# Weight buffers in the feed-forward: four raw and three split, in place of two and four, and pure blocks first in a seven-product piece

## The chip, the cores and the metric

One core of one Trainium2 chip runs the whole program. The metric is device time in microseconds (us) of one execution; lower is better. Engines are named as the profile names them: PE (TensorE, matmuls), PEld (its weight loads), DVE (VectorE), ACT (ScalarE), POOL (GpSimd) and SP (SyncE, which issues most transfers, its queue being written SPq). Every engine takes its instructions in a fixed order, laid down when the program is built.

## The reference

A decoder trunk of two layers on 256 tokens of width 2048, all in float32. Layer 0 mixes tokens with a diagonal state-space model and a gated linear unit, layer 1 with sliding-window attention; each is followed by a SwiGLU feed-forward of inner width 5632:

```python
def swiglu(x, w_gate, w_up, w_down):
    return (jax.nn.silu(x @ w_gate) * (x @ w_up)) @ w_down

for i in range(DEPTH):                       # DEPTH = 2
    hn = rmsnorm(h, norm_mix[i])
    mix = s5_mixer(hn, ...) if i == 0 else sliding_window_attention(hn, ...)
    h = h + mix
    hn = rmsnorm(h, norm_ffn[i])
    h = h + swiglu(hn, ffn_w_gate[i], ffn_w_up[i], ffn_w_down[i])
return rmsnorm(h, norm_final)
```

## The kernel before

**Pieces.** All large weights are read once, in pieces of 1 MB: four blocks of 128 x 512 float32. `W.src` lists the pieces in the order in which PE uses them (32 of the gated unit, 132 of the first feed-forward, 20 and 16 of the attention, 132 of the second feed-forward). A piece goes through two kinds of buffers. SP loads it into a *raw* buffer (`load`). ACT and DVE then split it into a high part rounded to fp32r and a low part, the rest (`split`), which lie in a *place*, a tile `w` of twice the size. A float32 product is three fp32r matmuls: x high with w high, x high with w low, x low with w high (`three`, `products`).

**Plain pieces.** `high` and `low` split a plain piece with one ACT instruction (L130) and one DVE instruction (L135). It feeds 24 matmuls.

**Seven-product pieces.** In gate and up a piece holds 2 x 2 blocks (two blocks of rows; up and gate). In about half of them the 2 x 2 block product is formed from seven block products instead of eight. `sevenths` makes four sums of blocks on DVE (`sf`, L144 to L146), splits these into the place `w` (L148 on ACT, L149 on DVE, in two halves), and splits three of the blocks themselves, the pure blocks, into a tile `sd` (L148, L149). There is one buffer `sd` and one buffer `sf`. Such a piece feeds 21 matmuls. `ORDER` sets the order of the seven products; m1, c11 and c12 read `sd`, the other four read `w`.

**Chunks.** A feed-forward is worked in 11 chunks of 512 inner columns. `gu(c)` does gate and up of a chunk in 8 pieces, numbered p0 to p7 here; from chunk 2 on p0, p2, p4 and p6 are seven-product pieces. `sums` and the lines after the loop then put the products together on DVE (L1213 to L1216, L1240, L1243, L1244), and the result `act` is transposed on DVE into `bt` (L1042), sent through DRAM by POOL, and split as `hT` (L1256 on ACT, L1257 on DVE). The down products of the group of chunks before lie between the chunks: 4 plain pieces after a chunk, d0 to d3 here, whose sums go into `h` (L1266). After chunks 0 and 1 there are none, and 12 stand at the end. One chunk with its downs is 12 pieces.

**Lookahead.** When PE's part of piece i is written, `next` has the splits written up to piece i + 3 in the feed-forward (i + 2 elsewhere) and the loads two pieces beyond. There are two raw buffers, and four places in the feed-forward (three elsewhere). The fourth place lies in the feed-forward's own pool `W.pool`. A build-time scheduler sorts what is ready into the fixed order of each engine, so that order is not quite that of the code.

Of the kernel before, what the change touches and what calls it, by code (L numbers as in the profile page):

```python
# [9 lines left out]
F32 = mybir.dt.float32  # L10
# [7 lines left out]
P = 128  # L18
# [40 lines left out]
def kernel(  # L59
# [9 lines left out]
    def nm(s):  # L69
        uid[0] += 1  # L70
        return f"{s}_{uid[0]}"
# [5 lines left out]
    pp = ctx.enter_context(tc.tile_pool(name="pp", bufs=4))  # L77
    wq = ctx.enter_context(tc.tile_pool(name="wq", bufs=2))
# [14 lines left out]
    class Weights:  # L93
# [11 lines left out]
        def load(self, upto):  # L105
            while len(self.raw) < min(upto, len(self.src)):
                i = len(self.raw)
                aps = self.src[i][0]
                t = pp.tile([P, 4, 512], F32, tag="raw", name=nm("raw"), bufs=2)
                v = t.rearrange("p (k s) n -> p s k n", s=len(aps))  # L110
                for s, ap in enumerate(aps):
                    nc.sync.dma_start(v[:, s], ap.rearrange("(a p) n -> p a n", p=P))  # L112
                self.raw.append(t)

        def place(self, i):

            if i in (1, 4):
                return self.third()
            if not self.src[i][2]:
                self.wide = None  # L120
                pool, n = (wp, 1) if i % 3 == 1 else (wq, 2)
            else:
                self.wide = i % 3 if self.wide is None else self.wide + 1
                pool, n = {1: (wp, 1), 3: (self.pool, 1)}.get(self.wide % 4, (wq, 2))
            return pool.tile([P, 2, 4, 512], F32R, tag="w", name=nm("w"), bufs=n)

        def high(self, i, keep=lambda ins: ins):
# [34 lines left out]
        def next(self):  # L162
            i = self.used
            self.used += 1
            n = 4 if self.src[min(i + 3, len(self.src) - 1)][2] and i + 3 < self.limit else 3
            self.split(min(i + n, self.limit))
            self.load(i + n + 2)
            return self.hl[i]

    W = Weights()  # L170
# [65 lines left out]
    def s5(early_piece):  # L236
# [3 lines left out]
        with st:  # L240
# [591 lines left out]
            def outputs(q, mms=(0, 1), keep=lambda ins: ins):  # L832
                for mm in mms:
                    for i in range(4):
                        for ri in range(2):
                            for h in range(2):
                                place = 8 * mm + 4 * h + i
                                for g2 in range(2):
                                    r = rows(g2)
                                    keep(PE.matmul(py[q][g2][h * NK : (h + 1) * NK, mm, i], St[q][r, ri, place],  # L840
                                                   Tt[q][r, place, ri].rearrange("p j c -> p (j c)"),
                                                   start=False, stop=mm == 1 and i == 3 and ri == 1))
                                    keep = lambda ins: ins
# [341 lines left out]
    def swiglu(norm, out_norm):  # L1185
# [3 lines left out]
        def three(acc, x_, w, first, last):  # L1189
# [3 lines left out]

        M = {"m1": ("a11", "b11"), "c11": ("a12", "b21"), "c12": ("s4", "b22"), "c21": ("a22", "t4"),
             "m5": ("s1", "t1"), "m6": ("s2", "t2"), "m7": ("s3", "t3")}
        ORDER = ("m1", "m6", "m7", "m5", "c11", "c21", "c12")

        def gu(c):
            acc = {}
# [3 lines left out]
            def to(m):  # L1203
                first = m not in acc
                if first:
                    acc[m] = bank([P, 512], "acc")
                return acc[m], first
# [10 lines left out]
            for p in range(8):  # L1218
                w = W.next()
                xt = norm.xt[p // 2]  # L1220
                if p in sv:
                    for m in ORDER:
                        a, first = to(m)
# [245 lines left out]
    wp = ctx.enter_context(tc.tile_pool(name="wp", bufs=1))  # L1469
# [11 lines left out]
    glu(n0)  # L1481
    n1 = Norm(1, (), (0, 1, 2, 3))
    swiglu(n0, n1)
    ffn.close()
    n2 = Norm(2, (0, 1, 2, 3))
    attention(n1, n2, ffn_pool)
    swiglu(n2, Last(None))
    ffn.close()

# [27 lines left out]
```

## Time and profile before

| | us |
|---|---|
| median of 3 runs | 2003.87 (2003.23 to 2007.51) |
| profiled execution, its own time | 2004.44 |
| its span in the trace | 2002.3 |
| PE, DVE, ACT busy | 1909.4, 1594.4, 1001.8 |
| first feed-forward, first to last matmul | 295.45 to 1024.25 |
| second feed-forward, first to last matmul | 1259.85 to 1993.35 |

The span begins with the state-space part and the gated unit (to 295 us); the attention lies between the two feed-forwards. A row of the trace begins with the start in us and the duration; "idle before" is how long the engine stood still, with the instruction that released it. Matmuls overlap in the pipeline, so the time of one (389 ns) is longer than the step from one start to the next.

### The profile page before, as it was taken

The page shows a single profiled execution, that of the slowest core. Times are in us where ns is not written, and L with a number is a line of the kernel's source. Part 1 is how long each engine was busy: PE and PEld are TensorE (multiplying, and loading weights), DVE is VectorE, ACT ScalarE, POOL GpSimd, SP SyncE. Part 2 cuts the span into 40 slices and gives each one's busy share as a digit, 9 for nine tenths or more (in the row PEclk, how much of TensorE's full clock was granted, in tenths as well). Part 3 has the DMA queues.
Part 4 walks back from the last instruction along what each step waited for, and adds up shares of the span by engine and source line. Part 5 has one row for each costly group of instructions (what it writes and reads, how often), then busy time and mean ns, then how long its engine had stood idle before and what let it go on. Part 6 is the DMA issues. An engine that isn't in the chain of part 4 may idle for free.

```text
span 2002.3 us, 25614 instructions
## 1 busy us (share of the span) xinstructions
PE 1909.4 (95%) x10050; PEld 1556.1 (78%) x10050; DVE 1594.4 (80%) x1933; ACT 1001.8 (50%) x1061; POOL 217.6 (11%) x272
## 2 busy tenths in 40 slices
PE   7789999999999999999999999999999999999998
PEld 6678887877777777777888778877777877787786
DVE  8965568888888888888687887888888888888875
ACT  6554455454444544444465555645444444454443
POOL 6840000100000000000020111001000000000000
PEclk9799999999999999999999999999999999999999
DMA  4037775665566566655785866656666566755664
GB/s 129 24 103 235 241 225 190 228 229 190 192 229 214 186 199 221 214 185 196 242 277 185 265 207 230 213 203 222 206 209 227 173 210 210 225 177 202 215 227 151
DMA packets 201084, 405.76 MB, mean 203 GB/s; under 512 B 16418, under 2 KB 16482, under 8 KB 200836
## 3 DMA queue, kind: packets, MB, share of 16 engines
q1 hardware_dynamic: 185984, 356.88, 53.8%
q0 software_dynamic: 14144, 45.12, 7.0%
q10 hardware_dynamic: 836, 2.14, 0.3%
q8 instruction: 78, 1.28, 0.3%
q14 instruction: 42, 0.34, 0.1%
HBM read 379.45 MB, written 24.64 MB: 202 GB/s over the span
## 4 chain that ended last, share of the span: by engine, by line
DVE 32%; DMA 32%; PE 20%; ACT 10%; issue 5%; SPq 1%; POOL 0%; ACTq 0%; DVEq 0%; POOLq 0%
DMA raw<-in_ffn_w_gate_dram 19%; DVE w L135 13%; DMA raw<-in_ffn_w_down_dram 11%; ACT w L130 8%; PE acc L964 5%; PE acc L966 5%; PE acc L965 5%; DVE sd L149 4%; DVE w L149 3%; DVE sf L144 2%; SPq L112 1%; DVE scan L615 1%; ACT sd L148 1%; DVE sf L146 1%; DVE sf L145 1%
## 5 line engine op out<-in xcount | busy, mean ns | idle before, releaser
L135 DVE TENSOR_TENSOR w<-raw,w 128x2048 fp32r<-128x2048 f32 x248 | 570.1, 2299 | 222.3 <-ACT w L130 220.1
L130 ACT ACTIVATE w<-raw 128x2048 fp32r<-128x2048 f32 x250 | 478.7, 1915 | 406.9 <-DMA raw<-in_ffn_w_down_dram 174.7
L1191 PE MATMUL acc<-w,xT 128*128 128x512 f32 x1080 | 426.6, 395 | 27.7 <-DVE w L149 27.4
L1190 PE MATMUL acc<-w,xT 128*128 128x512 f32 x1080 | 424.0, 393 | 4.5 <-DVE u L1240 2.0
L148 ACT ACTIVATE w<-sf 128x1024 fp32r<-128x1024 f32 x164 | 172.3, 1052 | 301.7 <-DVE sf L144 288.1
L965 PE MATMUL acc<-w,hT 128*128 128x512 f32 x704 | 274.1, 389 | 1.1 <-DVE w L135 1.1
L1192 PE MATMUL acc<-w,xT 128*128 128x512 f32 x704 | 274.1, 390 | 0.0
L966 PE MATMUL acc<-w,hT 128*128 128x512 f32 x704 | 273.9, 389 | 0.0
L964 PE MATMUL acc<-w,hT 128*128 128x512 f32 x704 | 273.9, 389 | 0.0
L1191 PEld LDWEIGHTS acc<-w,xT 128*128 128x128 f32 x1080 | 204.3, 189 | 81.5 <-DVE w L149 39.5
L1036 POOL DMA_DIRECT2D pd<-bt x160 | 88.1, 554 | 1521.6 <-DVE bt L1042 1431.6
L1190 PEld LDWEIGHTS acc<-w,xT 128*128 128x128 f32 x1080 | 204.0, 189 | 53.0 <-ACT w L148 4.9
L149 DVE TENSOR_TENSOR w<-sf,w 128x1024 fp32r<-128x1024 f32 x164 | 199.6, 1219 | 1.8 <-ACT w L148 1.6
L144 DVE TENSOR_TENSOR sf<-raw 128x1024 f32<-128x1024 f32 x82 | 100.3, 1223 | 112.9 <-DMA raw<-in_ffn_w_gate_dram 112.9
L148 ACT ACTIVATE sd<-raw 128x1536 fp32r<-128x1536 f32 x82 | 121.3, 1480 | 113.8 <-DMA raw<-in_ffn_w_gate_dram 91.2
L965 PEld LDWEIGHTS acc<-w,hT 128*128 128x128 f32 x704 | 132.2, 188 | 29.3 <-DVE w L135 1.9
L1192 PEld LDWEIGHTS acc<-w,xT 128*128 128x128 f32 x704 | 132.4, 188 | 27.8
L964 PEld LDWEIGHTS acc<-w,hT 128*128 128x128 f32 x704 | 132.2, 188 | 27.4
L966 PEld LDWEIGHTS acc<-w,hT 128*128 128x128 f32 x704 | 132.2, 188 | 27.4
L1192 PE MATMUL acc<-w,xs 128*128 128x512 f32 x376 | 149.0, 397 | 0.0
L149 DVE TENSOR_TENSOR sd<-raw,sd 128x1536 fp32r<-128x1536 f32 x82 | 143.8, 1754 | 2.1 <-ACT sd L148 0.9
L1191 PE MATMUL acc<-sd,xT 128*128 128x512 f32 x246 | 99.0, 402 | 18.9 <-DVE sd L149 18.9
(281 smaller groups left out, 2676.2 us busy)
## 6 DMA issues: line engine op xcount, KB each, us to landing
raw<-in_ffn_w_up_dram SPq DMA_DIRECT2D x176, 512.0 KB, 3.9
raw<-in_ffn_w_gate_dram SPq DMA_DIRECT2D x176, 512.0 KB, 5.0
raw<-in_ffn_w_down_dram SPq DMA_DIRECT2D x88, 1024.0 KB, 5.1
raw<-in_s_w_glu_dram SPq DMA_DIRECT2D x32, 1024.0 KB, 5.3
raw<-in_attn_w_qkv_dram SPq DMA_DIRECT2D x20, 1024.0 KB, 5.4
pd<-bt POOLq DMA_DIRECT2D x136, 128.0 KB, 4.0
act<-pd POOLq DMA_DIRECT2D x34, 512.0 KB, 4.8
raw<-in_attn_w_o_dram SPq DMA_DIRECT2D x16, 1024.0 KB, 5.1
```

What stands on the lines that cost most here:

```text
L130: keep(S.activation(w[:, 0], self.raw[i], AF.Copy))
L135: keep(e.tensor_tensor(lo, self.raw[i], hi.bitcast(F32), op=ALU.subtract))
L144: V.tensor_tensor(f[:, 0:2], bc(r[:, 0], 1, 2), r[:, 1:3], op=ALU.subtract)
L148: S.activation(v[1], v[0], AF.Copy)
L149: V.tensor_tensor(v[2], v[0], v[1].bitcast(F32), op=ALU.subtract)
L964: keep(PE.matmul(acc, x_[:, 0], w[0][:, a], start=first, stop=False))
L965: PE.matmul(acc, x_[:, 0], w[1][:, a], start=False, stop=False)
L966: PE.matmul(acc, x_[:, 1], w[0][:, a], start=False, stop=last)
L1036: nc.gpsimd.dma_start(d[t].rearrange("(q k) e -> k q e", q=4), v[32 * t : 32 * t + 32])
L1190: PE.matmul(acc, x_[0], w[0], start=first, stop=False)
L1191: PE.matmul(acc, x_[0], w[1], start=False, stop=False)
L1192: PE.matmul(acc, x_[1], w[0], start=False, stop=last)
```

## The change

Three things change. `load` takes two more raw buffers, `rx`, from the feed-forward's pool: a feed-forward piece whose number leaves 2 or 3 when divided by 4 goes into `rx`, the others into `raw`. `place` has three places everywhere; the fourth is gone, and its space holds the two new raw buffers. `next` writes the splits up to piece i + 2 and, in the feed-forward, the loads up to piece i + 6. And `ORDER` puts the three products of `sd` near the front: m1, c11, c12, then those of `w`.

```diff
-                t = pp.tile([P, 4, 512], F32, tag="raw", name=nm("raw"), bufs=2)
+                if self.src[i][2] and i % 4 > 1 and self.pool:
+                    t = self.pool.tile([P, 4, 512], F32, tag="rx", name=nm("rx"), bufs=2)
+                else:
+                    t = pp.tile([P, 4, 512], F32, tag="raw", name=nm("raw"), bufs=2)
...
-            if not self.src[i][2]:
-                self.wide = None
-                pool, n = (wp, 1) if i % 3 == 1 else (wq, 2)
-            else:
-                self.wide = i % 3 if self.wide is None else self.wide + 1
-                pool, n = {1: (wp, 1), 3: (self.pool, 1)}.get(self.wide % 4, (wq, 2))
+            pool, n = (wp, 1) if i % 3 == 1 else (wq, 2)
...
-            n = 4 if self.src[min(i + 3, len(self.src) - 1)][2] and i + 3 < self.limit else 3
-            self.split(min(i + n, self.limit))
-            self.load(i + n + 2)
+            self.split(min(i + 3, self.limit))
+            n = 7 if self.src[min(i + 6, len(self.src) - 1)][2] else 5
+            self.load(i + n)
...
-        ORDER = ("m1", "m6", "m7", "m5", "c11", "c21", "c12")
+        ORDER = ("m1", "c11", "c12", "m6", "m7", "m5", "c21")
```

The lines of the changed kernel stand two lower in `swiglu` and in `sevenths` (L133 for L135, L147 for L149, L1264 for L1266), and its loads are L115 for L112.

Three places of the built order follow. The number at the end of a name is that of the tile. First DVE at the start of a chunk in the first feed-forward, from the h sums of the downs to the split of p2. Before, p0 is loaded into raw_457 and split into w_467 and sd_468, p1 is raw_463 and w_473, p2 is raw_470, w_475 and sd_476:

```order
L1266 TENSOR_TENSOR h_2219<-h_2219,acc_461_4526 128x512
L144 TENSOR_TENSOR sf_469_4568<-raw_457_4488 128x1024
L145 TENSOR_TENSOR sf_469_4568<-raw_457_4488,sf_469_4568 128x512
L149 TENSOR_TENSOR sd_468_4567<-raw_457_4488,sd_468_4567 128x1536
L146 TENSOR_TENSOR sf_469_4568<-raw_457_4488,sf_469_4568 128x512
L149 TENSOR_TENSOR w_467_4566<-sf_469_4568,w_467_4566 128x1024
L135 TENSOR_TENSOR w_473_4613<-raw_463_4530,w_473_4613 128x2048
L149 TENSOR_TENSOR w_467_4566<-sf_469_4568,w_467_4566 128x1024
L1257 TENSOR_TENSOR hT_459_4524<-act_465_4558,hT_459_4524 128x4x128 x2
L144 TENSOR_TENSOR sf_477_4645<-raw_470_4578 128x1024
```

After, p0 is raw_454 with w_471 and sd_472, p1 is raw_457 with w_475, p2 is rx_463 with w_477 and sd_478:

```order
L147 TENSOR_TENSOR w_471_4604<-sf_473_4606,w_471_4604 128x1024
L147 TENSOR_TENSOR sd_472_4605<-raw_454_4455,sd_472_4605 128x1536
L147 TENSOR_TENSOR w_471_4604<-sf_473_4606,w_471_4604 128x1024
L142 TENSOR_TENSOR sf_479_4677<-rx_463_4530 128x1024
L143 TENSOR_TENSOR sf_479_4677<-rx_463_4530,sf_479_4677 128x512
L144 TENSOR_TENSOR sf_479_4677<-rx_463_4530,sf_479_4677 128x512
L133 TENSOR_TENSOR w_475_4643<-raw_457_4488,w_475_4643 128x2048
L1255 TENSOR_TENSOR hT_409_4099<-act_415_4133,hT_409_4099 128x4x128 x2
L1264 TENSOR_TENSOR h_2219<-h_2219,acc_419_4177 128x512
L1264 TENSOR_TENSOR h_2219<-h_2219,acc_420_4178 128x512
L147 TENSOR_TENSOR w_477_4675<-sf_479_4677,w_477_4675 128x1024 x2
L147 TENSOR_TENSOR sd_478_4676<-rx_463_4530,sd_478_4676 128x1536
```

The sums `sf` of p2 now stand ahead of the split of p1 and of `hT`, and the last h sums behind `hT`; the split of `sd` in p2 is the last of its piece.

Second, the loads on SP from p6 of a chunk over the four downs to p1 of the next. Before:

```order
L112 DMA raw_441_4305<-in_ffn_w_up_dram 128x2x512
L112 DMA raw_441_4305<-in_ffn_w_gate_dram 128x2x512
L112 DMA raw_444_4336<-in_ffn_w_up_dram 128x2x512
L112 DMA raw_444_4336<-in_ffn_w_gate_dram 128x2x512
L112 DMA raw_448_4372<-in_ffn_w_down_dram 128x4x512
L112 DMA raw_450_4401<-in_ffn_w_down_dram 128x4x512
L112 DMA raw_452_4427<-in_ffn_w_down_dram 128x4x512
L112 DMA raw_454_4456<-in_ffn_w_down_dram 128x4x512
```

After:

```order
L115 DMA rx_430_4262<-in_ffn_w_up_dram 128x2x512
L115 DMA rx_430_4262<-in_ffn_w_gate_dram 128x2x512
L115 DMA rx_439_4296<-in_ffn_w_up_dram 128x2x512
L115 DMA rx_439_4296<-in_ffn_w_gate_dram 128x2x512
L115 DMA raw_444_4336<-in_ffn_w_down_dram 128x4x512
L115 DMA raw_446_4362<-in_ffn_w_down_dram 128x4x512
L115 DMA rx_450_4400<-in_ffn_w_down_dram 128x4x512
L115 DMA rx_452_4426<-in_ffn_w_down_dram 128x4x512
```

The order of the pieces is the same; the buffers go round in fours (raw, raw, rx, rx), so a load waits for the split of the piece four before it and not two before it.

Third, SP at the end of the attention, where the pool of the second feed-forward takes over the memory of the attention's tiles. Before, the loads of `w_o` run on to the last and those of the feed-forward follow. After:

```order
L115 DMA raw_1071_9378<-in_attn_w_o_dram 128x4x512
L115 DMA rx_1116_9696<-in_ffn_w_up_dram 128x2x512
L115 DMA rx_1116_9696<-in_ffn_w_gate_dram 128x2x512
L115 DMA raw_1075_9425<-in_attn_w_o_dram 128x4x512
L115 DMA rx_1118_9726<-in_ffn_w_up_dram 128x2x512
L115 DMA rx_1118_9726<-in_ffn_w_gate_dram 128x2x512
L115 DMA raw_1077_9454<-in_attn_w_o_dram 128x4x512
```

Two pieces of the feed-forward are loaded early there, and the 11th and 12th piece of `w_o` (raw_1075 and raw_1077) stand behind them on SP. The first of the two waits until the attention has read its tiles for the last time.

## The prediction

> **What bounds the kernel now.** I began with the busy times on the page and then looked at PE alone in the two feed-forwards, which take 1462 of the 2002 us. Columns after the stretch and its length: busy us of PE, PEld, DVE, ACT, POOL, then granted clock, DMA share, GB/s.
>
> ```profile
> PE 1909.4 (95%) x10050; PEld 1556.1 (78%) x10050; DVE 1594.4 (80%) x1933; ACT 1001.8 (50%) x1061; POOL 217.6 (11%) x272
> ...
> 200.00:290.00 90.00, 90.00 (x398) 74.51 (x397) 55.74 (x50) 44.96 (x44) 5.91 (x10) 1.00 0.73 234
> 295.45:1024.25 728.80, 702.39 (x3047) 571.24 (x3046) 600.47 (x544) 354.90 (x298) 46.46 (x81) 1.00 0.63 211
> 1259.85:1993.35 733.50, 706.39 (x3046) 572.86 (x3044) 595.99 (x546) 353.99 (x297) 35.52 (x60) 0.99 0.62 205
> ```
>
> PE looks 96% busy in the feed-forwards, so only 53.5 us (26.4 + 27.1) seem to be lost there. The timeline of PE says more, because it has the starts. These two rows are 67 matmuls apart, with no wait between:
>
> ```profile
> 599.77 0.39 PE L1191 MATMUL acc<-w,xT 128*128 128x512 f32 x1
> ...
> 614.95 0.39 PE L1192 MATMUL acc<-w,xT 128*128 128x512 f32 x1
> ```
>
> A fed PE starts one every 15.18 / 67 = 0.2266 us. A feed-forward has 41 seven-product pieces of 21 and 91 plain ones of 24 matmuls, 3045, so it needs 689.9 us. It takes 728.8 and 733.5: **38.9 + 43.6 = 82.5 us** are lost, 53.5 in waits that show and the rest in refilling after them and in slow stretches such as this one:
>
> ```profile
> 917.19 0.51 PE L1191 MATMUL acc<-w,xT 128*128 128x512 f32 x1 [2.02 <-DVE w L149]
> ...
> 919.13 0.63 PE L1191 MATMUL acc<-w,xT 128*128 128x512 f32 x1
> 919.56 0.63 PE L1192 MATMUL acc<-w,xs 128*128 128x512 f32 x1
> ```
>
> After a wait of 2.02 us the step is 0.43 us for a while, half speed. The Trainium skill ("Trainium Kernel Development and Optimization", Performance Expectations) calls matmul busy time a bad metric, as matmuls are pipelined, and LDWEIGHTS busy a good one. By its rule the loss comes from PEld: 74.51 / 90.00 = 0.828 is its share when fed, 571.24 and 572.86 us of it need 690.0 and 692.0 us, so 80.3 us are lost, near my 82.5 and far from the 53.5 of busy time.
>
> PE waits for DVE's splits, DVE and ACT wait for raw data, in the views of waits (us in total, times, longest):
>
> ```profile
> PE acc L1191 <- DVE w L149: 27.4, 20, 2.1
> PE acc L1191 <- DVE sd L149: 18.9, 14, 2.1
> ...
> PE acc L1190 <- DVE u L1240: 2.5, 2, 2.0
> ...
> PE acc L965 <- DVE w L135: 1.7, 3, 0.7
> ...
> DVE sf L144 <- DMA raw<-in_ffn_w_gate_dram: 112.9, 55, 4.1
> ...
> ACT w L130 <- DMA raw<-in_ffn_w_down_dram: 174.7, 78, 5.5
> ```
>
> The chain of waits around 600 us shows why the data is late, and the DVE timeline what it makes of the pace:
>
> ```profile
> 602.57 1.77 DVE sd L149
> 604.77 4.75 DMA raw<-in_ffn_w_gate_dram
> 609.64 1.24 DVE sf L144
> ...
> 663.16 1.23 DVE L144 TENSOR_TENSOR sf<-raw 128x1024 f32<-128x1024 f32 x1 [2.44 <-DMA raw<-in_ffn_w_gate_dram]
> ...
> 675.33 1.23 DVE L144 TENSOR_TENSOR sf<-raw 128x1024 f32<-128x1024 f32 x1 [2.89 <-DMA raw<-in_ffn_w_gate_dram]
> ```
>
> The split of `sd` ends, only then is its raw buffer free, the load takes 4.75 us, the next sums `sf` start when it lands. With two buffers this ring needs 12.17 us for a pair of pieces, a seven-product and a plain one, where PE needs 45 matmuls, 10.2 us. Neither bandwidth (DMA share 0.63) nor DVE (600.47 of 728.8, 82%) is full: the time is the latency of a ring with two buffers.
>
> **The change, part by part.** These rows price it (us busy, mean ns):
>
> ```profile
> L135 DVE TENSOR_TENSOR w<-raw,w 128x2048 fp32r<-128x2048 f32 x248 | 570.1, 2299 | 222.3 <-ACT w L130 220.1
> L130 ACT ACTIVATE w<-raw 128x2048 fp32r<-128x2048 f32 x250 | 478.7, 1915 | 406.9 <-DMA raw<-in_ffn_w_down_dram 174.7 <-DMA raw<-in_ffn_w_gate_dram 89.0 <-PE acc L966 64.8
> L148 ACT ACTIVATE w<-sf 128x1024 fp32r<-128x1024 f32 x164 | 172.3, 1052 | 301.7 <-DVE sf L144 288.1 <-DVE sf L146 13.6
> L149 DVE TENSOR_TENSOR w<-sf,w 128x1024 fp32r<-128x1024 f32 x164 | 199.6, 1219 | 1.8 <-ACT w L148 1.6
> L148 ACT ACTIVATE sd<-raw 128x1536 fp32r<-128x1536 f32 x82 | 121.3, 1480 | 113.8 <-DMA raw<-in_ffn_w_gate_dram 91.2 <-PE acc L1192 22.6
> L149 DVE TENSOR_TENSOR sd<-raw,sd 128x1536 fp32r<-128x1536 f32 x82 | 143.8, 1754 | 2.1 <-ACT sd L148 0.9
> L144 DVE TENSOR_TENSOR sf<-raw 128x1024 f32<-128x1024 f32 x82 | 100.3, 1223 | 112.9 <-DMA raw<-in_ffn_w_gate_dram 112.9
> L145 DVE TENSOR_TENSOR sf<-raw,sf 128x512 f32<-128x512 f32 x82 | 56.5, 688 | 1.9
> L1266 DVE TENSOR_TENSOR h<-h,acc 128x512 f32<-128x512 f32 x80 | 52.6, 679 | 3.8 <-PE acc L966 3.8
> L1244 DVE SCALAR_TENSOR_TENSOR act<-u,ry,act 128x512 f32<-128x512 f32 x44 | 31.1, 744 | 0.0
> L1042 DVE STREAM_TRANSPOSE bt<-act 128x1024 f32<-128x1024 f32 x22 | 27.3, 1239 | 0.1
> ```
>
> Nothing is added to any engine. The number of instructions and the bytes stay. DVE does for a chunk with its downs 4 seven-product splits (1.22 + 2 x 0.69 + 2 x 1.22 + 1.75 = 6.8 us), 8 plain ones (2.3), fourteen instructions of 128 x 512 at 0.68 (four sums, four sums more, two `hT`, four h sums), two of 0.74 and a transpose: 27.2 + 18.4 + 9.5 + 1.5 + 1.2 = 57.8 us. PE needs 276 x 0.2266 = 62.5. So DVE can keep PE fed, with 4.7 us to spare, if nothing makes it wait.
>
> Four raw buffers. A load now waits for the split four pieces back. At 5.2 us a piece (62.5 / 12) it has about 15 us from that split to its own, where it takes some 5:
>
> ```profile
> raw<-in_ffn_w_down_dram SPq DMA_DIRECT2D x88, 1024.0 KB, 5.1
> ```
>
> The ring no longer sets the pace, and the DMA and SPq steps leave the chain.
>
> Three places. The place of piece i is free when PE has ended piece i - 3; from there to the start of piece i are two pieces of PE, 10.2 us, in place of three. I walked DVE through the new order of a chunk, with t = 0 when PE starts p0 and p6 of the chunk before ending at -27.2. The sums start at -26.5, after ACT's copy. From there to the split of p2 DVE never waits, and the durations add up: four sums, d1, four sums, two of `act`, a third of `sf` for p0, d2, transpose, d3, a `sf`, two h sums, a `sf`, then the half of `w`, `sd`, the half of `w`: p0 is split at **-3.3**. Its place was free at -10.9 (d1's end), ACT is done before DVE. Then `sf` of p2 (2.6) and p1 (2.3): **1.6**, needed at 4.8. `hT` and two h sums (2.7), `w` of p2 (2.4, its place free at 0), `sd` of p2 (1.75): **8.6**, needed at 10.2. On, with short waits for ACT at p4 and for the places of p7 and d0, to p3 at 12.1 (15.0), p4 at 18.9 (20.4), p5 at 21.9 (25.2), p6 at 26.8 (30.6), p7 at 29.4 (35.4), d0 at 34.8 (40.8), each with its need in brackets; the sums of p6 start at 36.0, and -26.5 + 62.5 = 36.0: the walk closes. PE does not wait, with least to spare 1.6 and 1.5 us at the `sd` of p2 and p4. What is late next is thus a hand-over, not a buffer.
>
> Pure blocks first. `sd` has one buffer. In the old order its last reader was the last product, in the new one it is the third: 9 of 21 matmuls, so `sd` is free 12 x 0.2266 = 2.7 us earlier, and `w` is needed 2.0 us after the start, not 0.7. In the walk ACT splits `sd` for p2 from 2.9 and needs it free at 2.0; by the old order it would be free at 4.8, the `sd` split would end at 8.3 on the quickest path, and its 1.6 us would be nearly gone. So this part lets the three places do; by itself it removes at most the 18.9 us of `sd` waits, and at the least nothing.
>
> The chunk joins without downs. Chunks 0 and 1 are followed at once by the next chunk, all 8 PSUM banks are in use, and the fifth product of the new p0 must wait for the sums of c11 (the row of L1240). Walked likewise, DVE reaches these 1.8 us late at the join of chunks 1 and 2, and p2 behind it loses some 0.5; at the join of 0 and 1 the `sd` of p2 has 0.6 us to spare. I take 3 us in each feed-forward, between 0 and 5.
>
> The start of the second feed-forward. Two early loads stand ahead of two of `w_o` on SP, and likewise two ahead of loads of the gated unit. I cost all at nothing. The first waits for the attention's last read, the first row; the 11th `w_o` piece (raw_1075) behind it waits for the split of the 9th, the second row:
>
> ```profile
> 1204.96 0.39 PE L1418 MATMUL po<-pT,kv 128*64 128x128 f32 x4
> ...
> 1205.87 2.29 DVE L135 TENSOR_TENSOR w<-raw,w 128x2048 fp32r<-128x2048 f32 x1 [4.46 <-ACT w L130]
> ...
> 1216.33 0.39 PE L964 MATMUL acc<-w,oT 128*128 128x512 f32 x1
> ...
> 1227.21 0.39 PE L964 MATMUL acc<-w,oT 128*128 128x512 f32 x1
> ...
> 153.81 2.29 DVE L135 TENSOR_TENSOR w<-raw,w 128x2048 fp32r<-128x2048 f32 x1 [0.85 <-ACT w L130]
> ```
>
> So SP stands free at 1208.2 as now, and with 1 MB more ahead the 11th piece lands two loads later, at 1218.4 instead of 1213.3. Its place is free when PE begins the 9th piece (1216.33), its split needs 4.2 us, PE wants it at 1227.21: 4.6 us to spare. In the gated unit the 9th piece is split at 156.1 and wanted 24 pieces of 5.44 us before 295.45, at 164.9: it can take a load's delay too. If that cover is gone, one wait of up to 5 us each.
>
> Tail. Waits in the last 12 downs (the row of L965) I leave as they are, 2 us. Hand-overs between engines, which the walk sets to zero, can cost each of the 18 chunks from chunk 2 on between 0 and 1 us; the slack of 1.5 is nearer to zero, so 0.3, 5 us.
>
> **The sum.** 2004.4 (the profiled execution, 0.6 above the median) - 82.5 + 6 + 2 + 5 = 1934.9, and against the median **1934 us**. Its own range: 1921, if all the loss goes, to 1951, with the upper ends (10, 2 and 18 us).
>
> **The rivals.**
>
> Three places are too few (part of the gain). The walk adds durations; each ACT-to-DVE step also has a hand-over, and DVE is 92% loaded. If p2 and p4 each come 1 us late, with 20 chunks, 40 us are lost in place of the 5: 1969 us. For it: the margins of 1.6 and 1.5. Against: the gated unit runs with three places and two raw buffers, and from 200 to 290 PE is busy 90.00 of 90.00 us, though on plain pieces only.
>
> It does nothing (2004). The pace could be DVE's, with the raw wait only what fills its idle time. Against: DVE is at 82% in the feed-forwards, and `sf` waits 112.9 us for data.
>
> Slower, by the return of `hT`. ACT and DVE take `hT` between p0 and p2, in fixed order, and it comes through DRAM:
>
> ```profile
> 699.51 1.24 DVE L1042 STREAM_TRANSPOSE bt<-act 128x1024 f32<-128x1024 f32 x1
> ...
> 713.23 1.13 ACT L1256 ACTIVATE hT<-act 128x512 fp32r<-128x512 f32 x2
> ```
>
> The trip takes 12.5 us at most (700.75 to 713.23). In the walk `bt` ends at -12.6, so `hT` lands at 0; a trip of up to about 15 us is hidden, and beyond it each us delays ACT, the split of p2 and then PE, in 20 chunks. Loads up to four pieces deep could lengthen it. At 15 + 70 / 20 = 18.5 us the gain is gone; at 20 us the kernel takes 2034. Against: the loads are released one by one by the splits, and in the walk one or two are under way at that point, as now. The Trainium skill ("DMA: Bandwidth & Descriptors", Queues, rings and completion order) has each DMA engine go round between the queue rows packet by packet; by that rule POOL's transfers would at most share with the loads, a trip of twice the transfer time. No row here shows such a case with four loads queued.
>
> **How the numbers follow.** A difference under 0.2% (4 us) is about what a measurement of this kernel can't tell from none. Chances: the forecast 0.66, too few places 0.18, nothing 0.06, slower 0.10. Faster is 0.66 + 0.18 = 0.84, the same 0.05, slower 0.11 (a few of "nothing" fall there). The range of 1921 to 1978 holds the forecast and the first rival around its 1969.
>
> **What would show it.** Both feed-forwards at 692 to 700 us, PEld at about 82% there, the waits of L1191's successor (L1189) for `w` and `sd` from 46 to under 12 us, the wait of L144's successor for raw data from 113 to under 15, DVE at 86% in the feed-forwards, no stretch at half speed except at the chunk joins. Wrong would be: PE waiting for `sd` in p2 and p4 of most chunks (the first rival), ACT waiting for the data of `hT` (the third), or a DVE without waits and PE still starved (the second).

## The result, and the profile after

The changed kernel takes 1922.86 us (median; 1921.13 to 1923.50), beside 2005.69 us (2003.23 to 2008.11) for the kernel before on the same chip: a ratio of 0.9586, with a 95% interval of 0.9569 to 0.9602, some 83 us less. Beside the other kernels below it was run once more and took 1922.43 us, ratio 0.9594 (0.9572 to 0.9617). Against the prediction of 1934 us (1921 to 1978) that is 11 us faster than the forecast, and only 2 us inside the fast end of its range.

The busy times on the page, and the chain of waits as shares of the span by engine:

```profile
PE 1877.3 (98%) x10050; PEld 1551.6 (81%) x10050; DVE 1587.7 (83%) x1933; ACT 1006.4 (52%) x1061; POOL 217.8 (11%) x272
...
PE 91%; DVE 6%; ACT 1%; issue 1%; POOL 0%; DMA 0%; DVEq 0%; ACTq 0%
```

The chain is now PE's own, and DMA has left it. In the kernel before DVE and DMA held most of it:

```profile
DVE 32%; DMA 32%; PE 20%; ACT 10%; issue 5%; SPq 1%; POOL 0%; ACTq 0%; DVEq 0%; POOLq 0%
```

The table by stretch of the changed kernel, with the columns of the prediction, gives the gated unit and the two feed-forwards from their first to their last matmul:

```profile
200.00:290.00 90.00, 90.00 (x399) 74.53 (x398) 54.48 (x50) 44.06 (x43) 5.92 (x10) 1.00 0.72 235
293.68:983.88 690.20, 690.20 (x3046) 571.51 (x3045) 597.95 (x549) 360.07 (x302) 46.45 (x81) 1.00 0.67 220
1219.17:1910.32 691.15, 690.78 (x3046) 571.18 (x3044) 594.18 (x551) 356.45 (x297) 35.57 (x60) 1.00 0.64 215
```

The feed-forwards take 690.20 and 691.15 us where 3045 matmuls at the full pace need 689.9. Of the 82.5 us that were lost, 81.0 are back. The views of waits (us in total, times, longest) show what went and what came:

```profile
PE acc L1189 <- DVE sd L147: 0.3, 1, 0.3
...
DVE sf L142 <- DMA raw<-in_ffn_w_gate_dram: 11.4, 4, 4.4
...
ACT w L128 <- PE acc L964: 164.2, 56, 6.6
ACT w L128 <- PE acc L1190: 152.4, 77, 3.6
ACT w L146 <- PE acc L1190: 125.4, 37, 3.6
...
ACT hT L1254 <- DMA act<-pd: 48.9, 17, 4.4
```

PE's waits for splits fell from 46.3 us to 0.3, DVE's wait for raw data from 112.9 to 11.4. What ACT waits for now is mostly PE: a split can't begin until PE has left the place. The splits run as far ahead as three places allow, and it is PE that holds them up. Of the signs that the prediction named, PEld's share (82.8 and 82.6%), DVE's share (86.6 and 86.0%) and the waits came as said; the feed-forwards took a little less than the 692 to 700 us.

### The profile page after: what moved, and what is told of

Its sections match the earlier page's. It is cut to its first block, busy times and chain, and to the rows that moved or that the text cites. A ratio compares the mean times of both kernels' runs of the same rounds, so it can differ in the third digit from the quotient of the medians.

```text
span 1919.4 us, 25618 instructions
## 1 busy us (share of the span) xinstructions
PE 1877.3 (98%) x10050; PEld 1551.6 (81%) x10050; DVE 1587.7 (83%) x1933; ACT 1006.4 (52%) x1061; POOL 217.8 (11%) x272
## 4 chain that ended last, share of the span: by engine, by line
PE 91%; DVE 6%; ACT 1%; issue 1%; POOL 0%; DMA 0%; DVEq 0%; ACTq 0%
PE acc L1189 15%; PE acc L1188 15%; PE acc L1190 15%; PE acc L962 14%; PE acc L964 14%; PE acc L963 14%; DVE w L133 1%; DVE scan L613 1%; DVE V L618 1%; DVE V L616 1%; PE pv L250 1%; ACT sc L1373 0%; PE py L838 0%; PE pm L794 0%; PE px L250 0%
## 5 line engine op out<-in xcount | busy, mean ns | idle before, releaser
L133 DVE TENSOR_TENSOR w<-raw,w 128x2048 fp32r<-128x2048 f32 x156 | 358.5, 2298 | 165.6 <-ACT w L128 165.3
L128 ACT ACTIVATE w<-raw 128x2048 fp32r<-128x2048 f32 x158 | 302.9, 1917 | 348.8 <-PE acc L964 145.1
L146 ACT ACTIVATE w<-sf 128x1024 fp32r<-128x1024 f32 x164 | 168.4, 1055 | 221.4 <-PE acc L1190 125.4
L133 DVE TENSOR_TENSOR w<-rx,w 128x2048 fp32r<-128x2048 f32 x92 | 210.3, 2286 | 38.7 <-ACT w L128 38.1
L128 ACT ACTIVATE w<-rx 128x2048 fp32r<-128x2048 f32 x92 | 176.1, 1914 | 83.1 <-PE acc L1190 30.5
L147 DVE TENSOR_TENSOR w<-sf,w 128x1024 fp32r<-128x1024 f32 x164 | 196.1, 1220 | 26.5 <-ACT w L146 26.4
L963 PE MATMUL acc<-w,gt 128*128 128x512 f32 x256 | 99.7, 390 | 0.6 <-DVE w L133 0.6
L962 PE MATMUL acc<-w,gt 128*128 128x512 f32 x256 | 99.9, 391 | 0.0
```

The lines of the kernel that those rows point to most:

```text
L128: keep(S.activation(w[:, 0], self.raw[i], AF.Copy))
L133: keep(e.tensor_tensor(lo, self.raw[i], hi.bitcast(F32), op=ALU.subtract))
L146: S.activation(v[1], v[0], AF.Copy)
L147: V.tensor_tensor(v[2], v[0], v[1].bitcast(F32), op=ALU.subtract)
L962: keep(PE.matmul(acc, x_[:, 0], w[0][:, a], start=first, stop=False))
L963: PE.matmul(acc, x_[:, 0], w[1][:, a], start=False, stop=False)
```

## The experiments

All differ from the kernel before or the changed kernel by a few lines. First the three parts of the change were taken apart, with PE's loss in the two feed-forwards (first to last matmul, less 689.9 each) beside the times:

| kernel | raw buffers | places | order of products | us | ratio to before (95%) | lost in the two feed-forwards |
|---|---|---|---|---|---|---|
| before | 2 | 4 | old | 2003.87 | | 38.9 + 43.6 |
| order_alone | 2 | 4 | new | 1987.33 | 0.9915 (0.9885 to 0.9945) | 33.5 + 35.3 |
| look_three | 2 | 4, splits 3 ahead | new | 1990.37 | 0.9941 (0.9913 to 0.9969) | 31.9 + 29.4 |
| three_places | 2 | 3 | old | 1990.39 | 0.9920 (0.9895 to 0.9944) | 31.0 + 30.1 |
| two_raw | 2 | 3 | new | 1950.90 | 0.9730 (0.9695 to 0.9765) | 8.7 + 9.4 |
| old_order | 4 | 3 | old | 1944.33 | 0.9708 (0.9677 to 0.9738) | 8.2 + 12.1 |
| three_raw | 3 | 3 | new | 1923.77 | 0.9601 (0.9578 to 0.9625) | 1.0 + 2.9 |
| changed | 4 | 3 | new | 1922.86 | 0.9586 (0.9569 to 0.9602) | 0.3 + 1.3 |

Each ratio is to the kernel before as it ran beside that kernel on the same chip (medians of 2003.09 to 2005.69 us). The losses are those of the one execution that was profiled. In three kernels that execution was well under the median (two_raw 1942.39 us, old_order 1941.35, look_three 1986.61), so their typical loss is some 3 to 9 us larger.

**The order of products alone** (order_alone), in the kernel before:

```diff
-        ORDER = ("m1", "m6", "m7", "m5", "c11", "c21", "c12")
+        ORDER = ("m1", "c11", "c12", "m6", "m7", "m5", "c21")
```

> The kernel before with the new ORDER alone (two raw buffers, four places). Theory A, the ring of two raw buffers sets the pace: a pair of pieces still takes about 12 us for 10.2 us of PE, so the time stays near 2004 us, between 1990 and 2006; the waits of PE for sd may shrink, those for w or for the next piece grow. Rival B, the single sd buffer set the pace: the 18.9 us of sd waits and the half-speed stretches behind them go, 1975 to 1985 us.

16 us came, between what the two theories had expected. PE's wait for `sd` went from 18.9 us to 7.4, but a new one stands first among PE's waits of that kernel:

```profile
PE acc L1190 <- DVE h L1266: 25.0, 16, 3.3
```

PE waits for PSUM banks that the h sums must free, and on DVE these stand behind other work that waits. In the 9 us before nine of these 16 waits DVE had stood for raw data, before six for ACT's half of a plain split.

**The changed kernel with the old order** (old_order): the same line of the diff, backwards.

> The changed kernel with the old ORDER (four raw buffers, three places). Theory A, from the walk: sd is free 2.7 us later, so DVE takes the plain split of the next piece ahead of the sd split; that one ends after the place of p0, p2 or p4 is free plus 1.9 (ACT) plus 2.3 plus 1.75 us, 0.5 to 0.8 us too late at p2, p4 and p6; about 1.5 to 2 us a chunk in 20 chunks, 1950 to 1965 us, the waits of PE being for sd. Rival B, the order is idle decoration and four raw buffers do all: 1922 to 1928 us.

1944.33 us, some 21 more than the changed kernel: the order matters here, by less than the 1950 to 1965 us that were expected from the walk. One wait carries it, the `sd` wait that the prediction's walk named:

```profile
PE acc L1189 <- DVE sd L147: 13.0, 11, 2.1
```

It shows as 13.0 us of 20.3 lost; the rest is refilling after waits and steps that are longer than 0.2266 us. So the order is worth 16 us alone and 21 us on top of the rest.

**Two raw buffers in the changed kernel** (two_raw):

```diff
-                if self.src[i][2] and i % 4 > 1 and self.pool:
-                    t = self.pool.tile([P, 4, 512], F32, tag="rx", name=nm("rx"), bufs=2)
-                else:
-                    t = pp.tile([P, 4, 512], F32, tag="raw", name=nm("raw"), bufs=2)
+                t = pp.tile([P, 4, 512], F32, tag="raw", name=nm("raw"), bufs=2)
...
-            n = 7 if self.src[min(i + 6, len(self.src) - 1)][2] else 5
-            self.load(i + n)
+            self.load(i + 5)
```

> The changed kernel without the two rx buffers: two raw buffers, three places, new ORDER. Theory A, the raw ring: as slow as before or a little slower, since a place less is there too, 2000 to 2040 us, DVE's sums waiting some 100 us for raw data. Rival B, the order and the lookahead did it: below 1960 us.

This was the surprise: it takes 1951 us, so 52 of the 83 us come without any further raw buffer (the kernel before took 2003.09 us beside it). DVE's timeline of this kernel has the split of p7 of two chunks that follow each other, and a pair of pieces between, from one first sum `sf` to the next:

```profile
607.46 2.29 DVE L130 TENSOR_TENSOR w<-raw,w 128x2048 fp32r<-128x2048 f32 x1 [3.76 <-ACT w L125]
...
646.77 1.23 DVE L139 TENSOR_TENSOR sf<-raw 128x1024 f32<-128x1024 f32 x1 [0.70 <-DMA raw<-in_ffn_w_gate_dram]
...
657.39 1.23 DVE L139 TENSOR_TENSOR sf<-raw 128x1024 f32<-128x1024 f32 x1 [1.67 <-DMA raw<-in_ffn_w_gate_dram]
...
670.04 2.29 DVE L130 TENSOR_TENSOR w<-raw,w 128x2048 fp32r<-128x2048 f32 x1 [3.74 <-ACT w L125]
```

This chunk takes 62.58 us, PE's own pace of 62.5. The pair takes 10.62 us, where the kernel before took 12.17: still over PE's 10.2, but the four downs make it good. One pair says little, though: in the changed kernel, where PE is hardly ever short, the first pair of a chunk takes 13.2 us on average and the third 7.6. Safer are averages over the 18 chunks from chunk 2 on. The three pairs from p0 to p6 take 36.7 us in the kernel before, 33.5 in two_raw and 33.5 in the changed kernel, a whole chunk, from first sum to first sum, 66.7, 63.5 and 62.2. What two buffers cost is thus not one number; it hangs on the places and the order around them.

**Three raw buffers** (three_raw): `rx` with one buffer for the pieces whose number leaves 2 when divided by 3, and loads five pieces ahead.

```diff
-                if self.src[i][2] and i % 4 > 1 and self.pool:
-                    t = self.pool.tile([P, 4, 512], F32, tag="rx", name=nm("rx"), bufs=2)
+                if self.src[i][2] and i % 3 == 2 and self.pool:
+                    t = self.pool.tile([P, 4, 512], F32, tag="rx", name=nm("rx"), bufs=1)
...
-            n = 7 if self.src[min(i + 6, len(self.src) - 1)][2] else 5
+            n = 6 if self.src[min(i + 5, len(self.src) - 1)][2] else 5
```

> The changed kernel with three raw buffers in place of four (one rx, pieces taken in threes). Theory A, latency of a ring: a load waits for the split three pieces back, three pieces are 15.6 us of PE, the load takes 5.1 and the split of a seven-product piece some 7, so the ring still turns faster than PE: 1923 to 1935 us, with some waits for raw data on DVE and hardly any on PE. Rival B, each buffer gives an equal part of the gain: about 1963 us, halfway.

1923.77 us: the fourth raw buffer brings nothing that this measurement can tell.

**Which part of places and lookahead?** Two kernels filled the table: two_raw with the old order (three_places), and order_alone with the splits written three pieces ahead and the loads five, its four places kept (look_three):

```diff
-            n = 4 if self.src[min(i + 3, len(self.src) - 1)][2] and i + 3 < self.limit else 3
-            self.split(min(i + n, self.limit))
-            self.load(i + n + 2)
+            self.split(min(i + 3, self.limit))
+            self.load(i + 5)
```

> The kernel before with three places and the splits written three pieces ahead (i + 2), two raw buffers, old product order. With the new product order the same kernel took 1951 us. Theory A (the lookahead of the splits, not the number of raw buffers, made most of the loss: with four pieces ahead DVE's fixed order puts splits that still wait for data in front of the h sums and of the piece that PE needs next): well below before, 1960 to 1985. Theory B (three places help only together with pure blocks first, since sd is the tight tile): 1990 to 2010.

> The kernel before with the new product order and with four places as before, but the splits written three pieces ahead and the loads five, as in the changed kernel with two raw buffers. Four pieces ahead took 1987 us. Theory A (the lookahead sets DVE's order, the fourth place itself is harmless): 1940 to 1960, as with three places (1951). Theory B (the order of four pieces ahead is harmless, it is the place that matters, through which ACT is held back to PE's pace): 1975 to 1995.

With two raw buffers the parts do not add. Three places alone bring 13 us and the order alone 16, both 52; the shorter lookahead with four places brings no more than the order alone. So theory A, the lookahead by itself, fell, and the fourth place really costs some 39 us there (1990 against 1951). The timeline of look_three (rows of ACT and one of DVE) at p0 of a chunk shows a way in which it can:

```profile
634.77 1.04 ACT L148 ACTIVATE w<-sf 128x1024 fp32r<-128x1024 f32 x1
...
636.99 0.68 DVE L146 TENSOR_TENSOR sf<-raw,sf 128x512 f32<-128x512 f32 x1
...
638.81 1.92 ACT L130 ACTIVATE w<-raw 128x2048 fp32r<-128x2048 f32 x1 [2.99 <-DMA raw<-in_ffn_w_gate_dram]
640.63 1.04 ACT L148 ACTIVATE w<-sf 128x1024 fp32r<-128x1024 f32 x1
```

Between the two halves of `w` of a seven-product piece stands the split of the plain piece behind it, which waits 2.99 us for its data, and the second half, whose sums were ready at 637.67, waits with it. In the built order of ACT such a plain split stands between the halves in 42 of 82 seven-product pieces in the kernel before, 39 in order_alone, 36 in look_three, 26 in three_places, 18 in two_raw, 4 with three raw buffers (three_raw), and 4 and 2 with four (changed, old_order). The losses go in the same sequence, except old_order's, which is the `sd` wait, but not in proportion: 36 and 26 pieces go with 61.3 and 61.1 us, 18 with 18.1.

That is a correlation, so the last kernel (plain_behind) forced it: in look_three a copy of one column from the second half of `w` into the plain piece's place, ahead of its split.

```diff
             w = self.place(i)
+            if i and self.src[i - 1][1]:
+                S.activation(w[:, 0, 0, 0:1], self.hl[i - 1]["t4"][0][:, 0:1], AF.Copy)
             keep(S.activation(w[:, 0], self.raw[i], AF.Copy))
```

> Four places, two raw buffers, new product order, splits three pieces ahead (1990 us with the order as the scheduler laid it), and now a copy of one column from the second half of a seven-product piece's w into the place of the plain piece behind it, so that ACT must take that plain piece after the half. In the built order of the 1990 us kernel a plain split stands between the two halves of w on ACT in 36 of 82 seven-product pieces; here in none. Theory A (the loss with two raw buffers is mostly ACT waiting for the data of a plain piece while a half that could run stands behind it): 1935 to 1960, as with three places and two raw buffers (1951, 18 of 82). Theory B (the two raw buffers' ring itself, or the fourth place, sets the pace): 1980 to 2000; the 82 copies cost ACT some 0.2 us each and PE nothing.

1978.34 us, ratio 0.9861 (0.9836 to 0.9886): 12 us better than look_three and far from 1951. Between the halves no plain split stands any more, and yet 54.7 us are lost in the two feed-forwards. The time lies just under the range of theory B and far above that of theory A. Its waits (three of DVE, one of PE) show that the run traded one wait for others:

```profile
DVE w L137 <- ACT w L132: 201.2, 141, 5.2
DVE w L151 <- ACT w L150: 79.7, 71, 1.1
...
DVE sf L146 <- DMA raw<-in_ffn_w_gate_dram: 7.2, 6, 3.4
...
PE acc L1192 <- DVE w L137: 12.8, 33, 1.6
```

DVE hardly waits for raw data any more (7.2 us against 80.5 in look_three), but 71 times for ACT's half of `w` (79.7 against 23.6), and PE now waits 33 times for the split of a plain piece. DVE's order is another one here too, so the run changed more than the blocked half. The blocked half is likely a part of the loss; why the fourth place costs as much as 39 us with two raw buffers is not settled.

**How much slack has DVE?** The changed kernel with the last instruction of the `sd` split of p2 done twice from chunk 2 on, for the same data (dve_more):

```diff
+            self.nth = -1
...
+            self.nth += 1
+            if self.nth % 41 >= 5 and (self.nth % 41 - 5) % 4 == 1:
+                for _ in range(1):
+                    V.tensor_tensor(v[2], v[0], v[1].bitcast(F32), op=ALU.subtract)
```

> The changed kernel with the last instruction of the sd split of p2 done twice from chunk 2 on (same data, same result): 1.75 us more on DVE in 18 chunks, and in DVE's order the first sums of p4 (1.23) now stand ahead of it. The prediction's walk had that split end at 8.6 us, needed at 10.2: now 11.6, 1.4 late in 9 to 18 chunks, +13 to +40 us (1936 to 1963). By the trace of the changed kernel it ended at 5.8: now 8.6, no wait: 1920 to 1930.

1925.32 us (1924.49 to 1930.34). The feed-forwards take 691.9 and 692.8 us, 1.7 more each. DVE's timeline in one chunk, where PE started p0 at 628.48 (row of PE below), has the repeat as L152:

```profile
628.48 0.39 PE L1193 MATMUL acc<-sd,xT 128*128 128x512 f32 x1
...
633.52 1.75 DVE L148 TENSOR_TENSOR sd<-rx,sd 128x1536 fp32r<-128x1536 f32 x1
635.19 1.22 DVE L143 TENSOR_TENSOR sf<-raw 128x1024 f32<-128x1024 f32 x1
636.33 1.75 DVE L152 TENSOR_TENSOR sd<-rx,sd 128x1536 fp32r<-128x1536 f32 x1
```

It ends 9.6 us after the start of p0, needed at 10.2: later than the 8.6 expected, since DVE stood 0.9 us for `hT`, but in time. In two other chunks PE waited for the repeat, 0.5 us in all. So 32 us more work on DVE cost 3.

**More seven-product pieces** (more_sevens): if PE is the bound again, fewer matmuls should pay.

```diff
-EARLY_SEVEN = ((0, 4), (0, 2, 6))
+EARLY_SEVEN = ()
```

p0, p2, p4 and p6 of chunks 0 and 1 are then all seven-product pieces, 9 matmuls less in each feed-forward.

> The changed kernel with p0, p2, p4 and p6 as seven-product pieces in chunks 0 and 1 too: three pieces more in each feed-forward, each with 3 matmuls less. Theory A, PE is the bound and DVE has room: 2 x 3 x 3 x 0.2266 = 4.1 us less, about 1919 us. Rival B, DVE falls behind in the two chunks that have no downs behind them (each such piece costs DVE 4.5 us more): the gain is eaten by waits, 1922 to 1930 us.

1923.75 us, ratio 0.9649 (0.9623 to 0.9674) to a kernel before that took 1993.65 us on that chip: no gain over the changed kernel. By the table of stretches the feed-forwards take 691.58 and 690.73 us, though 4.1 us of matmuls are gone:

```profile
293.36:984.94 691.58, 689.54 (x3037) 569.32 (x3036) 607.88 (x562) 364.92 (x308) 46.45 (x81) 1.00 0.65 220
1220.98:1911.71 690.73, 689.74 (x3037) 569.15 (x3035) 603.40 (x566) 361.57 (x303) 35.56 (x60) 1.00 0.63 215
```

The timeline of PE has the new waits in chunks 0 and 1, such as 1.12 us for ACT's half of `sd` at 379 and 0.61 for DVE's `w` at 381: the chunk joins, which the changed kernel just passes.

**A longer return of `hT`** (long_trip, and longer_trip with two): one copy more, DRAM to DRAM, on POOL's queue.

```diff
+        if hop:
+            d2 = dp.tile([4, P, 384], F32, name=nm("pe"), tag="pe")[:, :, : v.shape[2]]
+            nc.gpsimd.dma_start(d2.rearrange("t p e -> p t e"), d.rearrange("t p e -> p t e"))
+            d = d2
```

> The changed kernel with one more copy from DRAM to DRAM on the way of act to hT: the trip grows from 12.5 to some 17 us (a step of 512 KB takes 4 to 5 us); the output stays the same. Theory A, hT stands in the fixed order of ACT and DVE: the walk gave 15 us of cover, and the measured pieces are 2.3 to 2.8 us earlier than the walk, so about 17.5 us; 0 to 1 us a chunk in 22 chunks, 1923 to 1945 us. Rival B, hT is off the path: 1923 us.

> The same with two more copies from DRAM to DRAM: a trip of some 22 us. Theory A: beyond a cover of 17.5 us each us delays the split of p2 and PE behind it, 4 to 5 us in each of 20 chunks, 2000 to 2030 us, slower than the kernel before or level with it. Rival B, hT is off the path: 1923 us.

1932.78 and 1969.40 us, the second well under the 2000 to 2030 expected. The feed-forwards of the profiled executions (1935.43 and 1973.10 us) take 691.6 and 701.6 us with one copy, 713.7 and 718.5 with two: 12 and 51 us more than in the changed kernel. From the end of `bt` to the start of ACT's `hT`, where ACT waited for it, the trip took 13.8 us on average in the changed kernel (17 chunks, 12.1 to 14.9), 18.7 with one copy more (21 chunks) and 24.3 with two (22 chunks). The views of waits of ACT and DVE, long_trip first, then longer_trip:

```profile
ACT hT L1258 <- DMA act<-pe: 68.3, 21, 6.6
...
DVE hT L1259 <- ACT hT L1258: 45.9, 18, 3.7
```

```profile
ACT hT L1258 <- DMA act<-pe: 146.9, 22, 10.1
...
DVE hT L1259 <- ACT hT L1258: 96.0, 22, 8.2
...
PE acc L1193 <- DVE w L133: 13.1, 7, 2.0
```

The mechanism of the third rival is real: ACT waits, DVE behind it, and at last PE. Its price is not what the prediction had. A trip of 18.5 us was to undo the whole gain, but with 18.7 only 12 us are lost, and with 24.3 us 51. The loss is not spread over the chunks either. With one copy the trip is as long in the first feed-forward as in the second (18.8 and 18.6 us), but the first loses 1.4 us more than in the changed kernel and the second 10.5. PE's waits of the two come to 8.8 us, of which 7.8 lie between 1228 and 1390 us, in the first four chunks of the second feed-forward, and the first of them is not for a split. In the other chunks trips of up to 21 us are hidden almost whole, in place of 15; why the start of the second feed-forward is so much tighter, these runs do not show. Two copies more still leave the kernel faster than before (ratio 0.9869, 0.9839 to 0.9899).

## Why the prediction was right, and where not

**The loss.** "82.5 us are lost" held: the feed-forwards fell to 1.6 us above the floor in sum. The profiled execution's 2004.4 less 82.5 is 1921.9, and 1922.86 was measured. The Trainium skill ("Trainium Kernel Development and Optimization", Performance Expectations) calls LDWEIGHTS busy a good metric and matmul busy time a bad one. The traces agree: PEld's share gave a loss of 80.3 us and PE's busy time 53.5, and in the trace after that share is 571.51 / 690.20 = 0.828 in a feed-forward that PE fills, as in the fed stretch (74.53 / 90.00).

**The additions that did not come.** The sum had 13 us on top, 6 for the chunk joins, 2 for the tail, 5 for hand-overs; the feed-forwards show 1.6 us of them in all. The term mis-sized is the 13 us, and behind it the walk of DVE, which came out late for two reasons. These rows of DVE in the changed kernel belong to the chunk whose p0 PE starts at 627.56:

```profile
600.01 0.68 DVE L1211 TENSOR_TENSOR u<-u,acc 128x512 f32<-128x512 f32 x1
600.79 0.69 DVE L1212 TENSOR_TENSOR u<-u,acc 128x512 f32<-128x512 f32 x1
...
602.19 0.68 DVE L1214 TENSOR_TENSOR u<-u,acc 128x512 f32<-128x512 f32 x1
602.79 2.28 DVE L133 TENSOR_TENSOR w<-raw,w 128x2048 fp32r<-128x2048 f32 x1
604.99 1.28 DVE L1238 TENSOR_TENSOR u<-u,acc 128x512 f32<-128x512 f32 x2
...
620.89 1.22 DVE L147 TENSOR_TENSOR w<-sf,w 128x1024 fp32r<-128x1024 f32 x1
...
631.62 1.75 DVE L147 TENSOR_TENSOR sd<-rx,sd 128x1536 fp32r<-128x1536 f32 x1
```

The first sum starts at -27.55, where the walk had -26.5: it needs only m1 and m6, and did not wait for the end of p6 (-27.2), behind which the walk had put it. That is 1.05 us. And the walk added up durations, while most instructions that follow back to back start 0.08 us before the end of the one before in the record: one of 0.68 us (602.19) is followed after 0.60, one of 2.28 (602.79) after 2.20. So p0 was split at -5.45 (the walk: -3.3) and `sd` of p2 ended at 5.81 (the walk: 8.6, needed at 10.2); the second reason makes the other 1.7 us there. The slack at p2 was 4.4 us and not 1.6. That fits three places being enough, and dve_more, which used 3.8 us of it and cost little. That it also saved the chunk joins is likely, but the joins were not walked again.

**The ring of two raw buffers.** Here the step "with two buffers this ring needs 12.17 us for a pair" failed as a rule, though its sum came out. What it measured was the ring with the order and the places of that kernel: 36.7 us for three pairs. With three places and the new order the same two buffers take 33.5, and 52 of the 83 us are gone. That the buffers were held by splits that stood late in DVE's and ACT's order is the likely reading, and plain_behind shows it for a part at most. With four raw buffers, either order of products leaves at most 20.3 us above the floor, with two the combinations lie between 18.1 and 82.5 us above it. The forecast of the whole did not hang on this step: it took away all that PE lost, whichever part of the change did it. So the number came right although the prediction gave too much of the gain to the raw buffers.

**Pure blocks first.** Priced at 18.9 us at most and nothing at least by itself; the runs gave 16 us alone, 39 with three places and two raw buffers (1990.39 to 1950.90), 21 with four.

**The start of the second feed-forward and the tail** were costed at nothing and at 2 us. The span outside the feed-forwards went from 2002.3 - 1462.3 = 540.0 us to 1919.4 - 1381.35 = 538.05: the early loads cost nothing that shows.

**The rivals.** Three places are not too few (the 0.3 us wait for `sd`). "It does nothing" is ruled out by the result, and that DVE set the pace by dve_more. The return of `hT` is near: ACT waits for it 17 times in the changed kernel, for 48.9 us, where the kernel before had 4 waits of 3.2 us in all, and PE does not feel it.

## What to carry to other kernels

Compute the floor of the engine that should be full from starts, not from busy time: here 2004.4 less the loss above that floor is 1921.9, within 1 us of what all parts together gave. Before a ring's latency is called the bound, change the order and the places around it and leave the ring as it is; here that alone brought 52 us. Look for an instruction in the fixed order that waits for data and holds up others. The gains of such parts do not add, and each is priced with the others in place: 13 us and 16 us alone made 52 together, and the two further raw buffers added 28. In a walk through an engine's order use start-to-start times, and measure the slack by putting in work before calling a step tight.

## What the runs showed of the hardware

Vector instructions back to back mostly start 0.08 us before the recorded end of the one before, 2.20 us for one of 2.28. The Trainium skill ("VectorE: DVE Perf Modes", The DRAIN you can't avoid) says that a following instruction that is not held starts before the pipe of the one before is empty; the rows fit that and give the size. It does not hold for every pair: the sum at 600.79 reads what the one at 600.01 wrote, and starts 0.10 us after its end.

A copy of `act`'s transposed chunk (512 KB) from DRAM to DRAM on POOL's queue lengthened the trip by 4.9 us, a second by 5.6 more (13.8, 18.7, 24.3).
